# The first projection's matmuls as two row halves of the array, fifteen matmuls apart

## The chip, the cores and the metric

The kernel runs on one core of a Trainium2 chip. The metric is the time of one execution on the device in microseconds (us): the median of three runs of the kernel before is 665.21 us, the lowest 665.0 and the highest 665.22.

## What is computed

One decoder layer on 2048 tokens of width 1024 in float32: an RMS norm, one input projection to 2816 columns, two mixers side by side on its pieces (retention in chunks, and softmax attention in a window of 128 keys), a gate on each, an output projection, and the residual.

```python
h = rms_norm(x, norm_w)
proj = jnp.einsum('bsd,de->bse', h, w_in)
rq, rk, rv, rg, sq, sk, sv, sg = jnp.split(proj, offsets, axis=-1)
ro = group_norm(retention(rotary(rq), rotary(rk), rv)) * silu(rg)
so = sliding_window_attention(sq, sk, sv, q_norm_w, k_norm_w, sinks, rel_bias) * silu(sg)
x = x + jnp.einsum('bse,ed->bsd', concatenate([ro, so]), w_out)
```

The lines on the group norm and the concatenation stand here in short form.

## The kernel before

**Four large products.** The input projection is done in three pieces, of 2 x 512, 2 x 384 and 2 x 512 columns, and the output projection is a fourth of 2 x 512 columns. In the code they are the four calls of `products`, with the weights W2, W1, W3 and W4; "the first projection" is the call with W2 (lines 1585 to 1588). The 2048 tokens form eight pairs p of two chunks of 128 tokens. For each pair the product is a 2 x 2 by 2 x 2 block product (two token chunks and two halves of the contraction, times two halves of the contraction and two column halves), and it is made by Winograd's variant of Strassen's method, with seven block products m = 1 to 7 in the place of eight. So each call makes 7 x 8 = 56 block products.

**One block product.** A block product contracts over 512 rows in four steps k of 128, the height of the array. Each operand is split in two `fp32r` tiles, `hi` (the rounded value) and `lo` (the rest), and each step takes three matmuls: x hi by w hi, x hi by w lo, x lo by w hi (function `passes`). That makes 12 matmuls of 128 x 128 stationary values, 512 moving columns in the first projection, all into one PSUM bank, `acc`. ScalarE (ACT) makes `hi`, VectorE (DVE) makes `lo`. The results are combined by ACT and DVE out of PSUM: copied or added to sums in SBUF (`s`, `u`, `t`, `r`), lines 801 to 845. For m = 2 and m = 4 the matmuls go on in the bank in which m = 1 or m = 7 of the same pair lies.

**The order.** Class `Turns` lists the 56 block products of a call: the steps ((1, 2), (6), (5), (7, 4), (3)), within a step the pairs in groups of four (`FOURS`, the first projection), three (`THREES`, the output projection) or two (`TWOS`), within a group m by m. The place in the list is the block product's turn. Each operation is given to `Program.op` with what it reads and writes, its cost on the engine, and a due time in turns; `Program.emit` then takes operations one after another, for the engine that is free first, by due time and by free buffers, and writes each engine's queue in that order. `SHARE` says how many 512-wide tiles or PSUM banks each kind of buffer may hold at once: 11 for the split x (`x`), 19 for the split weights (`wh`), 5 banks for the first projection's `acc` (`first`). A buffer named `turn` is written by every block matmul, so that they stay in the list's order.

**The first eight turns.** Turns 0 to 3, (1, 0) to (1, 3), are written out with other tiles (`opening`), since they start while x is still being loaded; turns 4 to 7, (2, 0) to (2, 3), follow in the ordinary form. With 12 matmuls to a turn these are 96 matmuls. Turns 8 to 55 are 48 block products, 576 matmuls.

**What else TensorE does.** After the first projection, smaller matmuls stand between the block matmuls: transposes with `ident`, the attention logits (`m<-ks,qT`, tiles of 64 rows by 32 columns of the array), the attention values (`m<-pT,vn`, 32 by 64) and the retention steps (`m<-v,qk` and others, 64 by 64). These run in parts of the array, several at a time, and are in fp32: the profile shows each as two matmuls. None of them lies inside the first projection.

**GpSimd (POOL).** It makes only the factors of the attention's q and k norms, in two chains of sixteen small operations (`qk_norms`, lines 1310 to 1326), the first of which is due at turn 50.5.

Of the kernel before, what the change touches and what calls it, by code (L numbers as in the profile page):

```python
# [39 lines left out]
P = 128  # L40
NCH = S // P
NP = NCH // 2
HALF = P // 2
# [20 lines left out]
SHARE = {"x": 11, "raw": 92, "acc": 58, "wr": 28, "wh": 19, "att": 17, "ret": 35, "rin": 87, "gate": 25, "mix": 53, "norm": 14, "res": 7, "turned": 18, "vn": 3, "first": 5, "block": 3, "rest": 6}  # L64

AHEAD_OF = {"x": 5.0, "wh": 8.0}

# [17 lines left out]
OPENING = 4  # L85
SEM = 0.06
# [55 lines left out]
class Program:  # L142
# [5 lines left out]
    def op(self, cost, go, r=(), w=(), due=0.0, table=None, label="", also=(), many=0):  # L148


        o = Op()
        o.cost, o.go, o.due, o.after, o.set, o.label, o.many = cost, go, due + SHIFT.get(label, 0.0), [], table, label, many * MORE
        o.n, o.left, o.ready, o.end, o.seen, o.by = len(self.ops), 0, 0.0, 0.0, 0.0, None
        deps = set()
        for b in r:
            if b.writer is not None:
                deps.add(b.writer)
        for b in w:
            if b.writer is not None:
                deps.add(b.writer)  # L160
            deps.update(b.readers)
        for b in r:
            b.readers.append(o)
        for b in w:
            b.writer, b.readers = o, []
        o.bufs = list(dict.fromkeys((*r, *w, *also)))
        for b in o.bufs:
            b.left += 1
        o.new = [b for b in (*w, *also) if b.ap is None and b.tag]
        for d in deps:  # L170
            if d is not o:
                d.after.append(o)
                o.left += 1
        self.ops.append(o)
        return o
# [200 lines left out]

def f32r(n, count):
    t = count * (n / 2400 + 0.0135)
    return {"T": (t, t + 0.2, False)}


# [46 lines left out]
def layer(ctx, tc, xt, xfirst, xtok, nw, w_in, w_rn, qkw, sinks, biasg, rope, decays, dmask, gpow, w_out, out):  # L428
# [19 lines left out]
    op = prog.op  # L448
# [13 lines left out]
    def ps(share="rest", name="m"):  # L462
        return Buf("bank", None, F32, name, share)
# [51 lines left out]
    wr = fixed([P, 4], "wr")  # L515
# [237 lines left out]


    turn = Buf(name="turn", ap=())

    def products(B, W, n, base, seq, sink, plus=None, opening=None):


        s, u, t, bank = {}, {}, {}, {}  # L760

        def passes(m, acc, xh, xl, cols, k, d, goes_on, parts, which):


            wh, wl = W[m][k]

            def go(e):
                for i in which:
                    a, b = ((xh, wh), (xh, wl), (xl, wh))[i]
                    e.matmul(  # L770
                        acc()[:, :n], a()[:, cols], b()[:, :n], start=(not goes_on and k == i == 0),
                        stop=(k == 3 and i == 2), skip_group_check=goes_on,
                    )
# [3 lines left out]
            op(f32r(n, len(which)), go, reads, [acc, turn], d, label=f"product {m}", also=(xh, xl, wh, wl),  # L777
               many=2 * len(which))

        for m, p in seq.all:  # L780
            d = base + seq.at[m, p]
            goes_on = m in (2, 4)
            if plus and (m, p) == seq.all[-1]:
                last_product(B[m, p], W[m], d, t[p], p)
                break
            if not goes_on:
                bank[p] = ps("first" if opening else "block", "acc")
            acc = bank[p]
            if m > 1 or p >= OPENING or not opening:
                xh, xl = B[m, p]  # L790
                for k in range(4):
                    passes(m, acc, xh, xl, slice(k * P, (k + 1) * P), k, d, goes_on, (xh, xl), (0, 1, 2))
            elif p == OPENING - 1:
                for k, (xh, xl, parts) in enumerate(opening):

                    for which in ((0,), (1,), (2,)) if k < 3 else ((0, 1, 2),):
                        for q in range(OPENING):
                            due = (OPENING * k + q) / 4
                            passes(m, bank[q], xh, xl, slice(q * P, (q + 1) * P), k, due, False, parts[q // 2], which)

            def copy(dst, acc=acc, due=d - 3):
                op(
                    {"A": act(n)}, lambda e: e.activation(dst()[:, :n], acc()[:, :n], AF.Copy),
                    [acc], [dst], due, label="copy " + dst.name,
                )
                return dst

            def add(dst, a, acc=acc, due=d - 3):
                op(
                    {"V": dve(n)}, lambda e: e.tensor_tensor(dst()[:, :n], acc()[:, :n], a()[:, :n], ALU.add),  # L810
                    [acc, a], [dst], due, label="add " + dst.name,
                )
                return dst

            def more(dst, a, due):
                op(both(n), lambda e: e.tensor_tensor(dst(), dst(), a(), ALU.add), [dst, a], [dst], due, label="more")
                return dst

            if m == 1:
                if not opening or p >= OPENING:
                    s[p] = copy(kb("s", "acc"))
                elif p == OPENING - 1:
                    for q in range(OPENING):
                        s[q] = copy(kb("s", "acc"), bank[q], 2.6 + q)
            elif m == 2:
                r = plus(p, 0, 0, d) if plus else None
                sink(p, 0, 0, add(r, r) if plus else copy(kb("c", "acc")), d)
            elif m == 6:  # L830
                u[p] = add(s[p], s[p])
            elif m == 5:
                t[p] = add(kb("t", "acc"), u[p])
                if plus:
                    more(u[p], plus(p, 1, 0, d + 10), d + 10)
            elif m == 7:
                r = add(kb("r", "acc"), t[p])
                if plus:
                    r = more(plus(p, 1, 1, d), r, d + 1)
                    more(t[p], plus(p, 0, 1, base + seq.at[3, p] - 3), base + seq.at[3, p] - 3)  # L840
                sink(p, 1, 1, r, d)
            elif m == 4:
                sink(p, 1, 0, add(u[p], u[p]), d)
            else:
                sink(p, 0, 1, add(t[p], t[p]), d)

    def last_product(x, w, d, t, p):
# [717 lines left out]
    def go(e):  # L1565
        for _ in range(WARM):
            e.matmul(pw()[:, 0:256], zero.broadcast_to([P, P]), zero.broadcast_to([P, 256]), start=True, stop=True)
# [8 lines left out]
        label="no values",  # L1576
# [131 lines left out]
```

## Time and profile before

| | |
|---|---|
| median of three runs | 665.21 us (665.0 to 665.22) |
| span of the profiled execution | 663.5 us |
| TensorE (PE) busy | 658.8 us, 99% |
| its weight loads (PEld) | 562.3 us, 85% |
| VectorE (DVE) busy | 590.7 us, 89% |
| ScalarE (ACT) busy | 474.3 us, 71% |
| GpSimd (POOL) busy | 18.2 us, 3% |
| PE's granted clock, mean | 0.999 |

The profiled execution has a span of 663.5 us from its first to its last instruction; no total of its own is given for it, and the runs' median is 1.7 us above that span. PE is the matmul part of TensorE, PEld its weight loads, which overlap with matmuls. A row of the chain of waits gives start, length, what was done, and how many instructions; a row of the timeline the same with the engine first; a row of a table by window gives, for each engine, the busy time and in brackets the number of instructions that lie in it or touch it. Nearly every row names L424, the line of the helper through which each operation is issued, so groups are told apart by the tiles' names.

### The profile page before, as it was taken

Reading aid. Unit: us, or ns where it says so; the run is one execution under the profiler, and the core shown is the slowest. Engines: PE = TensorE matmul, PEld = TensorE weight load, DVE = VectorE, ACT = ScalarE, POOL = GpSimd, SP = SyncE. Lnnn points to the kernel's source line nnn. Section 1 sums busy time; section 2 is a strip of 40 time slices with the busy share of each in tenths; the row PEclk is TensorE's granted clock in tenths of the full one; section 3 lists DMA queues with packets and bytes.
Section 4 is the critical chain, followed back from the end, with each engine's and each line's share of the span. In section 5 each row is a group of like instructions: output and inputs, shape, how many; then the busy total and the mean of one; then the engine's idle time right before and its main releaser. Section 6 shows DMA issues by size and latency. Waiting matters only on the chain.

```text
span 663.5 us, 16277 instructions
## 1 busy us (share of the span) xinstructions
PE 658.8 (99%) x5952; PEld 562.3 (85%) x5952; DVE 590.7 (89%) x1369; ACT 474.3 (71%) x1154; POOL 18.2 (3%) x39
## 2 busy tenths in 40 slices
PE   9999999999999999999999999999999999999998
PEld 7888888889999999998878888877888888888887
DVE  6999977797799888899999999798999999998762
ACT  7665895567699676697999789899999863534200
POOL 0000000033300000000000000000000000000000
PEclk9999999999999999999999999999999999999999
DMA  9979997769949979999998999979977897146322
GB/s 319 385 234 314 317 324 252 241 211 332 220 156 284 276 230 310 286 295 313 296 214 255 256 263 259 244 211 258 299 238 218 226 198 215 45 162 212 137 95 96
DMA packets 152800, 160.86 MB, mean 242 GB/s; under 512 B 66704, under 2 KB 94224, under 8 KB 152720
## 3 DMA queue, kind: packets, MB, share of 16 engines
q1 hardware_dynamic: 152576, 159.81, 80.6%
q8 instruction: 47, 0.77, 0.5%
q14 instruction: 33, 0.27, 0.1%
q10 hardware_dynamic: 144, 0.00, 0.0%
HBM read 96.79 MB, written 49.09 MB: 220 GB/s over the span
## 4 chain that ended last, share of the span: by engine, by line
PE 99%; DMA 1%; ACT 0%; SPq 0%; DVE 0%; issue 0%
PE acc L424 88%; PE m L424 11%; DMA x<-in_xfirst 1%; ACT x L424 0%; SPq L424 0%; DVE t L424 0%
## 5 line engine op out<-in xcount | busy, mean ns | idle before, releaser
L424 PE MATMUL acc<-w,x 128*128 128x512 f32 (+1 forms) x2700 | 588.4, 377 | 0.9 <-ACT x L424 0.9
L424 PEld LDWEIGHTS acc<-w,x 128*128 128x128 f32 x2700 | 493.0, 188 | 84.4 <-issue 4.4
L424 DVE TENSOR_TENSOR x<-x 128x512 fp32r<-128x512 f32 (+2 forms) x220 | 143.6, 675 | 11.6 <-ACT x L424 10.5
L424 ACT ACTIVATE x<-x 128x512 fp32r<-128x512 f32 (+1 forms) x187 | 111.2, 620 | 21.3 <-DVE x L424 9.2
L424 ACT ACTIVATE lg<-lg,nm 128x160 f32<-128x160 f32 x128 | 53.1, 418 | 19.6 <-DVE nm L424 19.6
L424 DVE TENSOR_TENSOR w<-w 128x512 fp32r<-128x512 f32 (+3 forms) x96 | 61.1, 656 | 1.1 <-ACT w L424 1.1
L424 DVE SCALAR_TENSOR_TENSOR w<-w,nw_sb 128x512 fp32r<-128x512 f32 (+3 forms) x72 | 49.3, 702 | 0.9 <-ACT w L424 0.9
L424 DVE TENSOR_TENSOR s<-acc,s 128x512 f32<-128x512 f32 (+1 forms) x64 | 41.5, 649 | 8.3 <-PE acc L424 7.7
L424 ACT ACTIVATE w<-w 128x512 fp32r<-128x512 f32 (+1 forms) x72 | 41.3, 606 | 7.8 <-PE acc L424 5.1
L424 DVE CUSTOM_DVE_ANT_0 lg<-m,bias,nsnk 128x160 f32<-128x160 f32 x128 | 40.2, 379 | 2.3 <-PE m L424 2.2
L424 DVE TENSOR_TENSOR t<-acc,t 128x512 f32<-128x512 f32 (+2 forms) x33 | 21.0, 638 | 18.2 <-PE acc L424 18.0
L424 ACT ACTIVATE w<-w,nw_sb 128x512 fp32r<-128x512 f32 (+3 forms) x44 | 28.4, 691 | 3.3 <-DMA w<-in_w_in 2.3
L424 ACT ACTIVATE x<-go 128x512 fp32r<-128x512 f32 x27 | 16.8, 627 | 15.3 <-PE acc L424 7.5
L424 DVE TENSOR_TENSOR r<-acc,t 128x512 f32<-128x512 f32 (+1 forms) x32 | 20.8, 651 | 7.5 <-PE acc L424 7.2
L424 ACT ACTIVATE s<-acc 128x512 f32<-128x512 f32 (+1 forms) x32 | 18.3, 572 | 12.1 <-PE acc L424 11.5
L424 ACT ACTIVATE ro<-ro,nmu,rg 128x128 f32<-128x128 f32 x64 | 25.1, 481 | 2.1 <-DVE nmu L424 2.1
L424 DVE STREAM_TRANSPOSE pT<-lg 128x640 f32<-128x640 f32 x32 | 25.8, 825 | 0.9 <-ACT lg L424 0.9
L424 ACT ACTIVATION_READ_ACCUMULATOR lg<-lg,nm 128x1 f32 x128 | 24.3, 190 | 0.0
L424 DVE TENSOR_TENSOR t<-acc,s 128x512 f32<-128x512 f32 (+1 forms) x32 | 20.7, 645 | 3.8 <-PE acc L424 3.8
L424 ACT ACTIVATE xk<-xk 128x512 f32<-128x512 f32 x32 | 19.7, 620 | 4.3 <-DMA xk<-in_xtok 4.3
L424 ACT ACTIVATE qk<-qk,factors 128x64 f32<-128x64 f32 x64 | 16.9, 337 | 6.9 <-DVE qk L424 6.9
L424 ACT ACTIVATE ro<-m 64x256 f32<-64x256 f32 (+2 forms) x52 | 20.4, 392 | 0.6
(144 smaller groups left out, 590.6 us busy)
## 6 DMA issues: line engine op xcount, KB each, us to landing
x<-in_xt SPq DMA_DIRECT2D x80, 256.0 KB, 4.7
planes_dram<-apart SPq DMA_DIRECT2D x53, 256.0 KB, 3.6
x<-s_dram SPq DMA_DIRECT2D x46, 256.0 KB, 4.3
w<-in_w_in SPq DMA_DIRECT2D x40, 256.0 KB, 5.1
xk<-in_xtok SPq DMA_DIRECT2D x32, 256.0 KB, 4.9
res<-in_xtok SPq DMA_DIRECT2D x32, 256.0 KB, 3.5
s_dram<-x SPq DMA_DIRECT2D x23, 256.0 KB, 4.5
w<-in_w_out SPq DMA_DIRECT2D x20, 256.0 KB, 4.1
```

What stands on the lines that cost most here:

```text
L424: return lambda *a, **k: self.order.put(op(*a, **k))
```

## The change

In the first projection, from turn 8 to turn 55, each of the 576 block matmuls is issued as two matmuls, one on the upper 64 rows of the array (`rows` 1) and one on the lower 64 (`rows` 0), each over all 128 array columns and all 512 moving columns. A slot holds one upper matmul of the current block product and, fifteen matmuls behind it (`LAG`), one lower matmul of an earlier one. With 12 matmuls to a block product the lower half of a product starts three slots after its upper half has ended, so the two halves of a slot are always of different products and write to different banks. The upper half of a product clears the bank and the lower half adds to it. The first fifteen slots hold an upper half alone, and fifteen more slots at the end a lower half alone: 576 + 15 = 591 slots.

That the lower half of a product comes after its upper half is kept by a wait: a `nop` on GpSimd's queue (label `handed`) waits for the product's last upper matmul, and the first lower matmul waits for that `nop`. There are 48 of them.

Around it, the split weights get 20 tiles in the place of 19, and in the output projection's list the block product (3, 0) is moved ahead of (4, 6). Due times and costs being changed by this, `emit` puts some operations of later stages in other places as well. No operation is left out or added but the split matmuls and the `nop`s.

Three places in the queues, rows as the program has them (a name in brackets is the engine whose semaphore the instruction waits for; x9 stands for nine equal rows).

TensorE's queue at turn 8 of the first projection, before; `acc` is the bank, `w` and `x` the split operands:

```order
L424 MATMUL acc<-w,x 128x512 [waits Activation_49]
L424 MATMUL acc<-w,x 128x512
L424 MATMUL acc<-w,x 128x512 [waits DVE_49]
L424 MATMUL acc<-w,x 128x512 x9
L424 MATMUL acc<-w,x 128x512 [waits Activation_49]
```

The same place now:

```order
L436 MATMUL acc<-w,x 128x512 [waits Activation_49]
L436 MATMUL acc<-w,x 128x512
L436 MATMUL acc<-w,x 128x512 [waits DVE_49]
L436 MATMUL acc<-w,x 128x512 x9
L436 MATMUL acc<-w,x 128x512 [waits Activation_49]
L436 MATMUL acc<-w,x 128x512
L436 MATMUL acc<-w,x 128x512 [waits DVE_49]
L436 MATMUL acc<-w,x 128x512
L436 MATMUL acc<-w,x 128x512 [waits Pool_sequencer_49]
L436 MATMUL acc<-w,x 128x512 x16
L436 MATMUL acc<-w,x 128x512 [waits Activation_49]
L436 MATMUL acc<-w,x 128x512 x3
```

The first twelve are product 8's upper halves alone, then three upper halves of product 9; from there upper and lower halves alternate, and the first lower one has the new wait on GpSimd's sequencer. In all, 672 matmuls of 512 columns have become 1248 up to the first of 384 columns.

GpSimd's queue at the first chain of q and k norms (`hs` the sums of squares, `fac` the factors, `rqk0t` a scratch tile), before:

```order
L424 TENSOR_TENSOR hs_86<-hs_86,r_all 128x40 [waits DVE_49]
L424 TENSOR_SCALAR hs_86<-hs_86 128x40 [waits Pool_49]
L424 TENSOR_SCALAR fac_87<-hs_86 128x40 [waits Pool_49]
L424 TENSOR_TENSOR rqk0t<-fac_87 128x40 [waits Pool_49]
L424 TENSOR_TENSOR rqk0t<-rqk0t,hs_86 128x40 [waits Pool_49]
```

Now; a `nop` has no row of its own, its wait for PE stands with the next row:

```order
L436 TENSOR_TENSOR hs_86<-hs_86,r_all 128x40 [waits PE_49,DVE_49]
L436 TENSOR_SCALAR hs_86<-hs_86 128x40 [waits Pool_49]
L436 TENSOR_SCALAR fac_87<-hs_86 128x40 [waits Pool_49]
L436 TENSOR_TENSOR rqk0t<-fac_87 128x40 [waits PE_49,Pool_49]
L436 TENSOR_TENSOR rqk0t<-rqk0t,hs_86 128x40 [waits Pool_49]
L436 TENSOR_SCALAR rqk0t<-rqk0t 128x40 [waits Pool_49]
L436 TENSOR_TENSOR fac_87<-fac_87,rqk0t 128x40 [waits PE_49,Pool_49]
```

So 44 of the 48 `nop`s stand ahead of the chain's first operation and the last four inside the chain, three or four operations apart.

TensorE's queue in the output projection (`go` a gated result that is turned, `pT` and `vn` the attention weights and values), before:

```order
L424 MATMUL acc<-w,x 128x512 x42
L424 MATMUL m<-ident,go 128x128 x8
L424 MATMUL acc<-w,x 128x512 x9
L424 MATMUL m<-pT,vn 64x128 x32
L424 MATMUL m<-pT,vn 64x256 x8
L424 MATMUL m<-pT,vn 64x128 x32
L424 MATMUL acc<-w,x 128x512 x111
```

Now:

```order
L436 MATMUL acc<-w,x 128x512 x9
L436 MATMUL m<-pT,vn 64x128 x32
L436 MATMUL m<-pT,vn 64x256 x8
L436 MATMUL m<-pT,vn 64x128 x32
L436 MATMUL acc<-w,x 128x512 x63
L436 MATMUL m<-ident,go 128x128 x4
L436 MATMUL acc<-w,x 128x512 x492
```

The last attention values have moved from the start of this stage to 63 + 492 + 24 block matmuls ahead of the program's end (the last 24, of 384 and 128 columns, are unchanged).

The diff, cut to its core:

```diff
-SHARE = {"x": 11, ..., "wh": 19, ...}
+SHARE = {"x": 11, ..., "wh": 20, ...}
...
 class Turns:
-    def __init__(self, many):
+    def __init__(self, many, apart=False):
...
+        if apart:
+            self.all.remove((3, 0))
+            self.all.insert(self.all.index((4, groups[-1][0])), (3, 0))
...
-FOURS, THREES, TWOS = Turns(4), Turns(3), Turns(2)
+FOURS, THREES, TWOS = Turns(4), Turns(3, True), Turns(2)
...
+TILED = {0: (8, 56)}
+TILE_GAP = 0.0055
+LAG = 15
...
+        def piece(e, m, acc, x, cols, k, i, rows=None, goes_on=False, start=False, stop=False):
+
+            a, b = ((x[0], W[m][k][0]), (x[0], W[m][k][1]), (x[1], W[m][k][0]))[i]
+            r = slice(0, P) if rows is None else slice(rows * HALF, rows * HALF + HALF)
+            return e.matmul(acc()[:, :n], a()[r, cols], b()[r, :n], start=start, stop=stop, skip_group_check=goes_on or rows is not None)
...
+        def halves(slots, d):
...
+            for both_halves in slots:
+                for rows, j, q in both_halves:
+                    m, p = chain[j]
+                    x, w, (k, i) = B[m, p], W[m][q // 3], divmod(q, 3)
+                    made.append((j, q, (m, bank_of[j], x, slice(k * P, (k + 1) * P), k, i, rows, True,
+                                        rows == 1 and q == 0 and m not in (2, 4), rows == 0 and q == 11)))
...
+            def go(e):
+                for j, q, a in made:
+                    ins = piece(e, *a)
+                    if a[6] == 1 and q == 11:
+                        last[j] = ins
+                    elif a[6] == 0 and q == 0:
+                        behind(ins, last[j])
...
+        def handed(j, d):
+
+            def go(e):
+                ins = e.nop(nofuse=True)
+                behind(ins, last[j])
+                last[j] = ins
+
+            op({"G": (0.05, 0.2, False)}, go, [bank_of[j]], [relay], d, label="handed")
...
+            if first <= seq.at[m, p] < end:
+                j = seq.at[m, p] - first
+                bank_of.append(begin(m, p))
+                for q in (0, 3, 6, 9):
+                    of, k = range(q, q + 3), 12 * j + q - LAG
+                    halves([[(1, j, i)] + ([(0, *divmod(12 * j + i - LAG, 12))] if k >= 0 else []) for i in of], d)
+                    done(k + 2)
+                handed(j, d)
+                if j == len(chain) - 1:
+                    for k in range(12 * j + 12 - LAG, 12 * j + 12, 3):
+                        halves([[(0, *divmod(i, 12))] for i in range(k, k + 3)], d + 0.5)
+                        done(k + 2)
+                continue
```

`behind` adds a dependency with a semaphore between two instructions; `done` calls the code that empties a bank once its product's last lower matmul has been issued.

More of the change, by code (lines that the diff above doesn't have):

```diff
@@ L62 @@
 SMALL, COUNTS = 3, {"ms": 1, "rxt": 1, "rqk0t": 1, "rqk1t": 1, "state": 4, "sT": 2}
-SHARE = {"x": 11, "raw": 92, "acc": 58, "wr": 28, "wh": 19, "att": 17, "ret": 35, "rin": 87, "gate": 25, "mix": 53, "norm": 14, "res": 7, "turned": 18, "vn": 3, "first": 5, "block": 3, "rest": 6}
+SHARE = {"x": 11, "raw": 92, "acc": 58, "wr": 28, "wh": 20, "att": 17, "ret": 35, "rin": 87, "gate": 25, "mix": 53, "norm": 14, "res": 7, "turned": 18, "vn": 3, "first": 5, "block": 3, "rest": 6}
 AHEAD_OF = {"x": 5.0, "wh": 8.0}
@@ L378, in f32r, with tiled @@
     t = count * (n / 2400 + 0.0135)
+    return {"T": (t, t + 0.2, False)}
+def tiled(n, count):
+    t = count * (n / 2400 + TILE_GAP)
     return {"T": (t, t + 0.2, False)}
@@ L755, in layer, with behind, passes @@
     turn = Buf(name="turn", ap=())
+    relay = Buf(name="relay", ap=())
+    def behind(ins, other):
+        tc.add_manual_dep(
+            ins.ins, other.ins.name, mybir.DependencyInfo(mybir.DependencyClass.Sync, mybir.DependencyReason.DATA),
+            reason="one half of the rows after the other",
+        )
     def products(B, W, n, base, seq, sink, plus=None, opening=None):
         s, u, t, bank = {}, {}, {}, {}
-        def passes(m, acc, xh, xl, cols, k, d, goes_on, parts, which):
+        def piece(e, m, acc, x, cols, k, i, rows=None, goes_on=False, start=False, stop=False):
+            a, b = ((x[0], W[m][k][0]), (x[0], W[m][k][1]), (x[1], W[m][k][0]))[i]
+            r = slice(0, P) if rows is None else slice(rows * HALF, rows * HALF + HALF)
+            return e.matmul(acc()[:, :n], a()[r, cols], b()[r, :n], start=start, stop=stop, skip_group_check=goes_on or rows is not None)
+        def passes(m, acc, x, cols, k, d, goes_on, parts, which):
             wh, wl = W[m][k]
@@ L768, in go @@
                 for i in which:
[L769 to L773, printed above, removed]
+                    piece(e, m, acc, x, cols, k, i, None, goes_on, not goes_on and k == i == 0, k == 3 and i == 2)
             pairs = ((parts[0], wh), (parts[0], wl), (parts[1], wh))
@@ L776, in passes @@
             reads = list(dict.fromkeys(b for i in which for b in pairs[i]))
-            op(f32r(n, len(which)), go, reads, [acc, turn], d, label=f"product {m}", also=(xh, xl, wh, wl),
+            op(f32r(n, len(which)), go, reads, [acc, turn], d, label=f"product {m}", also=(*x, wh, wl),
                many=2 * len(which))
-        for m, p in seq.all:
-            d = base + seq.at[m, p]
[L782 to L799, printed above, removed]
@@ new lines, in halves @@
+        def halves(slots, d):
+            if not any(slots):
+                return
+            made, reads, writes = [], [], []
+            for both_halves in slots:
[4 more added lines that the diff above has]
+                                        rows == 1 and q == 0 and m not in (2, 4), rows == 0 and q == 11)))
+                    reads += (x[i == 2], w[i == 1])
+                    writes.append(bank_of[j])
+            def go(e):
[5 more added lines that the diff above has]
+                        behind(ins, last[j])
+            op(tiled(n, len(slots)), go, list(dict.fromkeys(reads)), [*dict.fromkeys(writes), turn], d,
+               label="product", many=2 * len(made))
@@ new lines, in handed, with done, begin @@
+        def handed(j, d):
[4 more added lines that the diff above has]
+            op({"G": (0.05, 0.2, False)}, go, [bank_of[j]], [relay], d, label="handed")
+        def done(k):
+            if k > 0 and k % 12 == 11:
+                finish(*chain[k // 12], bank_of[k // 12])
+        def begin(m, p):
+            if m not in (2, 4):
+                bank[p] = ps("first" if opening else "block", "acc")
+            return bank[p]
@@ L845, in products @@
                 sink(p, 0, 1, add(t[p], t[p]), d)
+        first, end = TILED.get(base // NP // 7, (len(seq.all), 0))
+        chain, bank_of, last = seq.all[first:end], [], {}
+        for m, p in seq.all:
+            d = base + seq.at[m, p]
+            if plus and (m, p) == seq.all[-1]:
+                last_product(B[m, p], W[m], d, t[p], p)
+                break
+            if first <= seq.at[m, p] < end:
[11 more added lines that the diff above has]
+                continue
+            acc, x, goes_on = begin(m, p), None, m in (2, 4)
+            if m > 1 or p >= OPENING or not opening:
+                x = B[m, p]
+                for k in range(4):
+                    passes(m, acc, x, slice(k * P, (k + 1) * P), k, d, goes_on, x, (0, 1, 2))
+            elif p == OPENING - 1:
+                for k, (xh, xl, parts) in enumerate(opening):
+                    for which in ((0,), (1,), (2,)) if k < 3 else ((0, 1, 2),):
+                        for q in range(OPENING):
+                            due = (OPENING * k + q) / 4
+                            passes(m, bank[q], (xh, xl), slice(q * P, (q + 1) * P), k, due, False, parts[q // 2], which)
+            finish(m, p, acc)
     def last_product(x, w, d, t, p):
```

1 line of the change is left out of this document (added).

## The prediction

> **What bounds the kernel now.** I read the page's busy shares first, then what TensorE waited for, then the chain of waits.
>
> ```profile
> PE 658.8 (99%) x5952; PEld 562.3 (85%) x5952; DVE 590.7 (89%) x1369; ACT 474.3 (71%) x1154; POOL 18.2 (3%) x39
> PE acc L424 <- ACT x L424: 0.9, 1, 0.9
> PE acc L424 88%; PE m L424 11%; DMA x<-in_xfirst 1%; ACT x L424 0%; SPq L424 0%; DVE t L424 0%
> ```
>
> TensorE is busy for 99% of the span, a block matmul waited once, for 0.9 us, and the chain that sets the end is TensorE's own work. So a microsecond taken from TensorE's stream comes off the time, unless something else is then late. What that stream costs is read from its uninterrupted stretches in the chain of waits (start, length, how many matmuls):
>
> ```profile
> 203.36 6.45 PE acc L424 x36
> 227.65 10.61 PE acc L424 x60
> 381.78 5.66 PE acc L424 x24
> 389.15 7.02 PE acc L424 x30
> ```
>
> The lower two are of 512 columns: six matmuls more take 1.36 us more, so one takes 226.7 ns, and 24 of them leave 5.66 - 5.44 = 0.22 us, which is what it costs to enter and leave work in parts of the array. The upper two are of 384 columns: 4.16 us for 24, 173.3 ns each. The difference, 53.4 ns for 128 columns, is 0.417 ns a column. So 512 columns stream for 213.4 ns, and each block matmul has **13.3 ns** on top, whatever its width. Only this part can shrink.
>
> The changed stretch is turns 8 to 55. Its end is found from the chain's first long piece, which holds the first projection and 24 matmuls of 384 columns, and ends at 161.95; less 24 x 0.173 and the 0.2 us of the change to the first transposition, that is 157.6 us, and 576 x 226.7 ns = 130.6 us earlier, 27.0, is the start. The windows:
>
> ```profile
> 5.19 156.76 PE acc L424 x696
> ...
> 27.04:80.00 52.96, 52.96 (x235) 43.89 (x234) 52.42 (x88) 34.79 (x76) 0.00 (x0) 1.00 0.88 294
> 80.00:157.60 77.60, 77.60 (x344) 64.28 (x343) 62.41 (x129) 52.27 (x129) 6.68 (x16) 1.00 0.81 274
> ```
>
> TensorE is busy in all of its 130.56 us, at full granted clock (1.00), and that is the 576 matmuls' own time: there is no wait in it.
>
> **The change, part by part.** *What goes:* 576 matmuls of 226.7 ns, 130.6 us.
>
> *What comes:* slots of two halves, if the halves run at the same time. Each half still streams 512 columns, so a slot is not under 213.4 ns. And the lag costs whole slots: fifteen with an upper half alone, fifteen with a lower half alone, so 576 + 15 = **591** slots. The fifteen extra ones cost 3.2 us by themselves. Since the halves stand in a part of the array, the stretch is entered and left once, another 0.22 us. The change gains only where the slot is under (130.6 - 0.2) / 591 = **220.6 ns**, that is, where the 13.3 ns shrink to under 7.2.
>
> No 64-row half over all columns in this number format is in the trace. The nearest rows are the retention steps: four tiles of 64 by 64 at a time, two row halves in different banks, a new weight load for each.
>
> ```profile
> 387.86 0.62 PE L424 MATMUL m<-v,qk 64*64 64x128 f32 x16
> 388.30 0.41 PE L424 MATMUL m<-qkT 64*64 64x64 f32 x16
> 388.53 0.62 PE L424 MATMUL m<-state,qkT 64*64 64x128 f32 x16
> ```
>
> From one row's start to the next, sixteen matmuls are four rounds of four: 0.44 / 4 = 110 ns for 128 columns, 0.23 / 4 = 57.5 ns for 64. The slope is 0.82 ns a column, about two column times of 0.417 for this format; that makes 106.8 and 53.4 ns of streaming, and 3 to 4 ns on top of a round. So row halves do run at the same time, and a round has little on top. It doesn't prove as much for the halves here, which stream twice as fast. I bound the slot from below by the 3 ns (216.4 ns) and from above by no shrinking at all (226.7). If what is on top goes with the rows of a tile, half of it is left, 6.6 ns. I take 4.9 ns, between 3 and 6.6, **218.3 ns**: 591 x 218.3 = 129.0, + 0.2 - 130.6 = **-1.4 us**. The ends: 591 x 216.4 + 0.2 - 130.6 = -2.5 us; 591 x 226.7 + 0.2 - 130.6 = +3.6 us.
>
> *The weight loads* double in number. What one costs alone shows at the end, where the stream is short:
>
> ```profile
> 659.18 1.28 PE L424 MATMUL acc<-w,x 128*128 128x128 f32 x10
> L424 PE MATMUL acc<-w,x 128*128 128x128 f32 x12 | 1.5, 271 | 0.0
> ```
>
> Ten matmuls from the first's start to the last's end, with a last one of 271 ns, leave (1.28 - 0.27) / 9 = 112 ns each, where 128 columns stream for 53: a load of 128 columns takes up to 112 ns of the array's time. Two in a row make 224 ns, over the stream. If the halves' loads can't overlap, the slot is 224 ns and the sum is 591 x 224 + 0.2 - 130.6 = +2.0 us. Against it: a round of the steps' 57.5 ns holds four loads of 64 columns. At half of 112 each these would take 224 ns one after another, so about four overlap, though over column halves too. The Trainium skill ("TensorE: Matmul & The Clock Gate", LDWEIGHTS) says that a load's time goes by columns and not by rows, 128 / 1.2 = 107 ns, so halving the rows shortens no load; that speaks against this change. By that figure two loads in a row are 213 ns, and the sum would stay at that of the stream. The trace agrees on the size, with its 112 ns.
>
> *The new wait.* The first lower half of each product waits for a `nop` on GpSimd, which waits for the product's last upper half. Behind it on TensorE stands everything. The rows that size it are a block matmul's mean time from start to end (392 ns), the last step of the chain, and GpSimd's first chain:
>
> ```profile
> L424 PE MATMUL acc<-w,x 128*128 128x512 f32 x2004 | 464.8, 392 | 0.9 <-ACT x L424 0.9
> 660.47 0.02 issue
> 660.50 0.29 DVE L424 TENSOR_TENSOR t<-acc,t 128x128 f32<-128x128 f32 x1 [0.73 <-PE acc L424]
> 143.06 0.55 POOL L424 TENSOR_TENSOR hs<-hs,r_all 128x40 f32<-128x40 f32 x1 [141.61 <-DVE hs L424]
> 143.70 0.54 POOL L424 TENSOR_SCALAR hs<-hs 128x40 f32<-128x40 f32 x1
> ...
> 150.47 0.50 POOL L424 TENSOR_TENSOR fac<-fac,rstd_all 128x40 f32<-128x40 f32 x1
> ```
>
> The last upper half starts in slot 11 and ends 0.39 us later; the lower one starts four slots after it, 0.87 us, and its weights should be loaded from one slot earlier, 0.65 us. That leaves 0.26 us for two hops. One hop is 0.03 us from TensorE to VectorE (660.47 to 660.50), and GpSimd takes 143.70 - 143.61 = 0.09 us to go on after its own result. Taking 0.03 + 0.09 + 0.03 = 0.15 us, it fits; I take nothing for it.
>
> *GpSimd's chain.* Four `nop`s stand between the operations of the first chain of norms, so TensorE waits if the chain is late, and the chain waits for TensorE. Three or four operations of some 0.46 us (sixteen from 143.06 to 150.47) are 1.9 us at most, and a turn of 12 slots is 2.6 us. The chain is faster than the turns, so TensorE doesn't wait. The chain itself now ends after the last turn, at the very end of the projection, not four us before. Its first reader on TensorE is a transposition 24 matmuls of 384 columns, 4.2 us, later; I take nothing.
>
> *Operands.* VectorE is busy 52.42 of 52.96 us between 27 and 80 us, and TensorE would ask for its work 3.8% faster. What covers this is its lead, seen at 65.12 us (27.04 + 14 turns of 2.72), where turn 22 begins:
>
> ```profile
> L424 DVE TENSOR_TENSOR x<-x x60: 415/679/693, 5.6 to 64.8; 128x512 f32<-128x512 f32 x30, 128x512 fp32r<-128x512 f32 x22, 128x256 fp32r<-128x256 f32 x8
> ```
>
> Of the split's second halves (fp32r), the eight small ones are turns 0 to 3 and the 22 large ones reach turn 25: over three turns, 8 us ahead. Twenty turns of 0.1 us and the 3.3 us for which tiles are now held longer don't use that up. If they did, the 240 slots before 80 us would gain nothing, 2.0 us less, and the sum would be +0.6.
>
> *Issue and SyncE's queue.* TensorE gets 1152 instructions more, a matmul and a load for each slot. The logits' stretch in the chain below holds 128 matmuls and their loads in 2.36 us, 18 ns a matmul; a slot of two needs 218 ns. In SyncE's queue the loads of the norm's tokens (`xk`) move behind some stores; before, the last is issued at 84.8 us, and the chain that needs their sums starts at 143.06. I take nothing for either.
>
> ```profile
> 201.00 2.36 PE m L424 x128
> L424 SPq DMA_DIRECT2D xk<-in_xtok x32: 327/382/1217, 48.3 to 84.8; - x32
> ```
>
> *The rest* is other places for the same work: the number of stretches in parts of the array is the same, so TensorE's own sum is too. The move of (3, 0) and of the last values can only add waits, and there were none.
>
> **The rivals.** *Nothing on top shrinks*: the 13.3 ns is the same at 512 and 384 columns, so it belongs to each matmul, and a half has it too. Then it is +3.6 us, 668.8. The tiled rounds speak against it. Chance 0.07.
>
> *The hop by GpSimd is late* (the other side): it decides from 0.26 us on, and each tenth beyond costs 48 x 0.1 = 4.8 us. At 0.1 us late it is -1.4 + 4.8 = +3.4, 668.6. For it: no row shows a TensorE wait on GpSimd. Against it: the hops above. Chance 0.07. Other new waits (operands, GpSimd's chain, the moved values): +0.6 to a few us, 0.07.
>
> *Loads in a row*, 224 ns: +2.0 us, 667.2, chance 0.05; partly overlapped, a slot of 219.5 to 222.8: within 0.2% of before, 0.10.
>
> *Halves in turn, not together*: twice 226.7 in 576 slots is 130 us more. Four tiles at once in a round of 110 ns speak clearly against it: 0.01.
>
> *The rounds' 3 ns hold here*: slots of 217.3 and less, -2.0 us and better, about 662.7 (the 3 ns end at -2.5). Chance 0.22.
>
> **How the numbers follow.** The forecast, slots of 217.3 to 219.5 ns and no new waits, has 0.41: -2.0 to -0.7 us, middle -1.4. The sum is against the profiled execution's span of 663.5 us, so 662.1; the runs' median lies 1.7 us above that span, and I add the change to it: 665.2 - 1.4 = **663.8 us**. A measurement of this kernel can tell about 0.2%, 1.3 us, from no change, so the forecast lies on that border, and half of it counts as faster. Faster: 0.21 + 0.22 = 0.43. Same: 0.20 + 0.10, and 0.04 of the other waits, 0.34. Slower: 0.07 + 0.07 + 0.05 + 0.01, and 0.03 of the other waits, 0.23. The range: below, -3.1 us, a slot of 215.4 (2 ns on top), 662.1; above, the loads in a row, 667.2. It leaves out the two rivals at +3.4 and +3.6, the halves in turn, and what lies beyond at either end, some 0.2 together.
>
> **What would show it.** The stretch from turn 8 should take some 129.2 us in place of 130.6, as 591 slots of about 218 ns: its first 384-column matmul at 156.3 us and not at 157.6. Fifteen matmuls at either end should stand alone at the same pace. TensorE's waits should show no GpSimd; GpSimd's first chain should end with the projection. Slots near 227 or 224, or a gap in each product's fourth slot, would make the prediction wrong.

## The result, and the profile after

The changed kernel takes **672.63 us** (median of four runs, 671.91 to 673.06), the kernel before beside it 665.22 us. The ratio is 1.0105, with a 95% interval of 1.0088 to 1.0122: 1% slower, where 663.8 us and a range up to 667.2 were forecast. The profiled execution took 672.75 us with a span of 671.0 us, 7.5 us more than before.

The busy shares and what TensorE waited for (us in total, times, longest), after:

```profile
PE 664.3 (99%) x6528; PEld 584.7 (87%) x6528; DVE 594.0 (89%) x1370; ACT 476.2 (71%) x1153; POOL 14.3 (2%) x39
```

```profile
PE m L436 <- DVE state L436: 1.1, 1, 1.1
PE m L436 <- issue: 0.8, 1, 0.8
...
PE acc L436 <- ACT x L436: 0.6, 2, 0.4
PE acc L436 <- DVE x L436: 0.3, 1, 0.3
```

TensorE is still busy for 99%, and its busy time has grown by 5.5 us (658.8 to 664.3). No row names GpSimd, but three kinds of wait are new: one for VectorE's `state`, one with no releaser ("issue"), and two for operands (of ACT's two, one stood at the start before).

**The changed stretch.** By windows, from the first half at 27.25 us to the first 384-column matmul at 161.17 us:

```profile
27.25:161.17 133.92, 133.92 (x1153) 130.39 (x1153) 116.90 (x216) 87.61 (x203) 4.67 (x16) 1.00 0.81 271
```

No wait, full clock, and 133.92 us for 591 slots: **226.6 ns a slot**, the old pace, not 218.3. The first 384-column matmul comes at 161.17 and not at 156.3; before, it came at 157.6. The timeline has the pace of halves in pairs (upper row of the fence) and of lower halves alone at the end:

```profile
39.85 110.49 PE L436 MATMUL acc<-w,x 64*128 64x512 f32 x972
157.89 3.35 PE L436 MATMUL acc<-w,x 64*128 64x512 f32 x14
```

972 halves are 486 pairs; less a matmul's own 0.39 us and the 0.17 us by which the second half of a pair follows the first, (110.49 - 0.39 - 0.17) / 485 = 226.7 ns a pair. Fourteen alone: (3.35 - 0.39) / 13 = 228 ns each. So two halves do run at the same time, as forecast, and one half alone takes as long as two, or as a whole matmul.

**GpSimd's chain**, three rows of it with the idle time ahead of them:

```profile
150.13 0.26 POOL L436 TENSOR_TENSOR rqk0t<-fac 128x40 f32<-128x40 f32 x1 [1.49 <-PE acc L436]
152.85 0.26 POOL L436 TENSOR_TENSOR rqk0t<-fac 128x40 f32<-128x40 f32 x1 [1.44 <-PE acc L436]
...
159.25 0.25 POOL L436 TENSOR_TENSOR fac<-fac,rstd_all 128x40 f32<-128x40 f32 x1
```

It waits for TensorE at the `nop`s and ends at 159.5 us, with the projection, as forecast; nobody waits for it.

**After the first projection** 671.0 - 161.17 = 509.8 us follow, where there were 663.5 - 157.6 = 505.9: 3.9 us more, for the same work. The timeline shows three places. The retention step at 431 us, after and then before:

```profile
431.18 0.67 PE L436 MATMUL m<-v,sT 64*64 64x128 f32 x16
431.67 0.62 PE L436 MATMUL m<-v,qk 64*64 64x128 f32 x16
432.11 0.41 PE L436 MATMUL m<-qkT 64*64 64x64 f32 x16
432.33 0.62 PE L436 MATMUL m<-state,qkT 64*64 64x128 f32 x16
434.06 0.63 PE L436 MATMUL m<-ident,ro 128*128 128x128 f32 x4 [1.10 <-DVE state L436]
```

```profile
433.22 0.62 PE L424 MATMUL m<-state,qkT 64*64 64x128 f32 x16
433.77 5.73 PE L424 MATMUL acc<-w,x 128*128 128x512 f32 x24
```

Before, block matmuls followed the step. Now transpositions do, in banks that VectorE still has to empty, and TensorE stands for 1.10 us. The chain of waits has what VectorE was at, and ACT's eleven operations on `ro` that it had waited for:

```profile
424.90 4.35 ACT ro L436 x11
...
431.98 1.20 DVE w L436 x2
433.18 0.40 DVE sT L436 x2
433.58 0.34 DVE state L436
433.92 0.14 issue
434.06 0.63 PE m L436 x4
```

Two splits of weights (`w`, 1.20 us) stand ahead of `sT` and `state` in VectorE's queue. That they are what makes the step late is read from this chain; no run moves them alone. The second place is the last attention values, 144 matmuls, after and then before:

```profile
533.02 2.22 PE L436 MATMUL m<-pT,vn 32*64 32x128 f32 x118
536.08 0.68 PE L436 MATMUL m<-pT,vn 32*64 32x128 f32 x26 [0.84 <-issue]
```

```profile
478.89 2.54 PE L424 MATMUL m<-pT,vn 32*64 32x128 f32 x144
```

3.74 us in the place of 2.54, with a stop of 0.84 us that nothing shown in the profile released. The third is the output projection, where two stops for operands of 0.38 and 0.27 us cost some 0.27 us more each: the overlap with the next matmul is lost (0.16 us: 0.39 less 0.23), and the first one after a stop takes 0.34 us to the next one's start (0.73 - 0.39 in the first row below), 0.11 longer than usual.

```profile
543.48 0.73 PE L436 MATMUL acc<-w,x 128*128 128x512 f32 x2 [0.38 <-ACT x L436]
544.49 1.88 PE L436 MATMUL acc<-w,x 128*128 128x512 f32 x7 [0.27 <-DVE x L436]
```

That is 1.2 for the values, 1.1 to 1.2 for the step and 1.2 for the operands, 3.5 to 3.6 of the 3.9 us.

### The profile page after: what moved, and what is told of

Its sections match the earlier page's. It is cut to its first block, busy times and chain, and to the rows that moved or that the text cites. A ratio compares the mean times of both kernels' runs of the same rounds, so it can differ in the third digit from the quotient of the medians.

```text
span 671.0 us, 17495 instructions
## 1 busy us (share of the span) xinstructions
PE 664.3 (99%) x6528; PEld 584.7 (87%) x6528; DVE 594.0 (89%) x1370; ACT 476.2 (71%) x1153; POOL 14.3 (2%) x39
## 4 chain that ended last, share of the span: by engine, by line
PE 92%; DVE 4%; ACT 2%; DMA 1%; issue 1%; SPq 0%; ACTq 0%
PE acc L436 83%; PE m L436 10%; ACT ro L436 1%; DVE x L436 1%; DVE w L436 1%; DVE st L436 0%; DMA w<-in_w_in 0%; DVE t L436 0%; DMA v<-aq_dram 0%; DVE go L436 0%; DVE state L436 0%; SPq L436 0%; ACT w L436 0%; DVE sT L436 0%; DVE tcos L436 0%
## 5 line engine op out<-in xcount | busy, mean ns | idle before, releaser
L436 PE MATMUL acc<-w,x 128*128 128x512 f32 (+2 forms) x3276 | 593.1, 378 | 0.9 <-ACT x L436 0.6
L436 PEld LDWEIGHTS acc<-w,x 128*128 128x128 f32 (+1 forms) x3276 | 515.4, 187 | 67.1 <-issue 4.7
L436 PE MATMUL m<-pT,vn 32*64 32x128 f32 (+1 forms) x1152 | 20.6, 285 | 0.8 <-issue 0.8
L436 PEld LDWEIGHTS m<-pT,vn 32*64 32x64 f32 x1152 | 18.4, 130 | 3.1 <-issue 1.8
```

The costliest lines, as they stand in the source:

```text
L436: return lambda *a, **k: self.order.put(op(*a, **k))
```

## Experiments

Two theories stand against each other for the stretch. **Per matmul:** what lies on top of the stream belongs to each matmul in a row of matmuls, whatever part of the array it uses, so halves can't shrink it. **Per phase or load:** it is made by loads or by the way in which the two halves follow each other, and could still be had. For the later 3.9 us: waits from the new order of the queues, against a consequence of the halves themselves.

### The halves put together again: a_full

All queues of ACT, VectorE, SyncE and GpSimd as in the changed kernel; TensorE issues whole matmuls in the place of the halves.

```diff
-                    ins = piece(e, *a)
-                    if a[6] == 1 and q == 11:
-                        last[j] = ins
-                    elif a[6] == 0 and q == 0:
-                        behind(ins, last[j])
+                    if a[6] == 1:
+                        ins = piece(e, *a[:6], None, True, a[8], q == 11)
+                        if q == 11:
+                            last[j] = ins
```

> The changed kernel's queues on VectorE, ScalarE, GpSimd and SyncE instruction by instruction, but TensorE's 576 block matmuls issued at full height (each where its upper half stood, the lower halves left out; the same result is computed). Main theory: each half keeps the 13.3 ns on top, so a slot is 226.7 ns and the halves cost 15 extra slots plus one entry, 3.6 us; so turns 8 to 55 go back to 130.6 us, and the time falls by at least 3.6 us, to 669.0 or less. What is left over 665.2 is the other order of the queues: 1.2 us of a retention step that waits for VectorE stays. The wait of 1.1 us inside the last attention values and the operand waits of 1.0 us after it stay if the order causes them (669.0), and go if they hang on where the reload of TensorE's instructions falls, since 1152 instructions less shift it by half a piece (about 666.5). Rival, the halves alone cost all of it: 665.2.

It took 668.33 us, 1.0044 of before (1.0028 to 1.0061): 4.3 us under the changed kernel, and 3.3 us above before. The window from the first changed matmul to the first of 384 columns:

```profile
27.55:158.11 130.56, 130.56 (x577) 108.15 (x576) 115.09 (x214) 87.85 (x202) 4.94 (x13) 1.00 0.83 278
```

```profile
PE m L436 <- DVE state L436: 1.1, 1, 1.1
PE m L436 <- issue: 0.9, 1, 0.9
...
PE acc L436 <- ACT x L436: 0.6, 2, 0.4
PE acc L436 <- DVE x L436: 0.3, 1, 0.3
```

The stretch is 130.56 us again, to the hundredth, and the later waits are still there, the one without a releaser in an earlier stretch of values (at 217.53 us and not at the last). The traced execution is the slowest of the four, 670.1 us. So the loss has two parts: the halves, 3.4 us in the stretch, and the order of the queues.

### 128 more instructions ahead: f_shift

```diff
-        for _ in range(WARM):
+        for _ in range(WARM - 2):
...
+        for _ in range(34):
+            e.matmul(pw()[0:32, 0:1], zero.broadcast_to([P, 32]), zero.broadcast_to([P, 1]), start=True, stop=True)
```

The extra matmuls stand ahead of everything and move the place of each later one in TensorE's instruction stream.

> The changed kernel with all queues as they are, but 128 TensorE instructions more ahead of the first block matmul (34 tiny warm-up matmuls in the place of two large ones), which moves every later reload of instructions by half a piece. Theory: the 1.1 us wait in the last attention values (named issue by the profile) is a reload that falls into them; it goes, and with it most of the 1.0 us for which two block matmuls wait for their operands just after: 670.3 or a little more if the start is later. Rival, the wait has to do with the values' own inputs: no change, 672.5.

It took 674.48 us (1.0142, 1.0127 to 1.0158). TensorE's waits, and the timeline's row for the last values:

```profile
PE m L436 <- DVE state L436: 1.1, 1, 1.1
...
PE acc L436 <- ACT x L436: 0.4, 1, 0.4
PE acc L436 <- DVE x L436: 0.3, 1, 0.3
```

```profile
535.55 2.56 PE L436 MATMUL m<-pT,vn 32*64 32x128 f32 x144
```

The stop without a releaser is gone and the values take 2.56 us. Some 2 us less were expected of the whole, and it takes 1.9 us more than the changed kernel: the longer warm-up puts the first changed matmul at 29.82 us in the place of 27.25, while what follows the projection falls from 509.8 to 508.5 us.

In the kernel with whole matmuls, which has 576 instruction pairs less, the stop stood in another stretch of the values (at 217.53 us, 0.94 us). What fits both is that TensorE ran out of instructions in a burst of short ones. The 16 KB packets of the instruction queue q8 become more with TensorE's instructions: 47 before, 51 in the changed kernel, 52 here. In the two bursts that stop, such a packet starts 0.65 and 0.11 us after the burst's start; in none of the other 94 bursts of values in the traces of this case does one start within the first microsecond. But the place in the instruction stream does not decide it alone: j_bf16 and j_cols64 below have the whole matmuls' queue on TensorE, and the same burst runs through in 2.53 and 2.54 us. So with one trace of each kernel it is not shown that the 128 instructions are what removed the stop. The waits for `state` and for the operands stayed, so the operand waits were no consequence of that stop.

### The true price in the plan: c_price

```diff
-TILE_GAP = 0.0055
+TILE_GAP = 0.0133
```

The plan reckons with 5.5 ns on top of each slot; here it reckons with 13.3. The instructions are the same, in the order that follows from the slower slots.

> The changed kernel planned with the measured price of a slot (13.3 ns on top in the place of 5.5), so that the order is made for the times that occur. Theory that the later waits come from an order made for a TensorE 4.7 us faster than it is: they go, and only the slots' 3.6 us are left, 668.8. Rival, any new order of this size brings waits of its own: anywhere from 668.8 to 673.

It took 668.83 us (1.0055, 1.004 to 1.007).

```profile
27.39:161.39 134.00, 134.00 (x1153) 131.53 (x1153) 117.65 (x218) 87.24 (x202) 5.63 (x16) 1.00 0.80 270
```

```profile
PE m L436 <- PEq L1774: 0.8, 1, 0.8
PE acc L436 <- ACT x L436: 0.3, 1, 0.3
```

The stretch is as long as in the changed kernel and all later waits are gone; what is left is of the start. Behind the projection 667.4 - 161.39 = 506.0 us follow, where there were 505.9 before. So the halves by themselves cost 3.8 us (3.4 in the stretch, and some tenths at the start, which differs from run to run: the first changed matmul stood between 26.6 and 27.7 us in runs with the same opening). That is the rival "nothing on top shrinks". The other 3.8 us, 672.63 - 668.83, came with the order that was planned at 5.5 ns. e_phase below, planned at 5.5 ns too, has waits of the same kinds (0.7 us for `state`, 5.5 us for operands, the start's 0.5 among them); the three d kernels, planned without halves, have none of the three. That the wrong price as such makes the waits, and not the chance of one order, rests on these six orders, and in e_phase the hop disturbs the plan as well.

### The other two edits alone: d_untiled, d_apart, d_wh20

```diff
-TILED = {0: (8, 56)}
+TILED = {}
```

That is the first; the second has 19 tiles for the split weights as well, the third leaves (3, 0) where it was.

> No block matmul is split; the change's two other edits stay (20 tiles for the split weights, the block product (3, 0) moved ahead in the output projection), and the order of the queues is planned for that. If these two edits cost nothing by themselves, and the waits seen after the change come from a plan that reckons with slots that are too fast, the time is that of the kernel before, 665.0 us, within 1 us. If one of the two edits makes waits (the operand waits stand in the output projection, where the second edit acts), it is 666 to 668, with a wait for operands at about 537 us.

> The kernel before with the block product (3, 0) of the output projection moved ahead, and nothing else. If this move makes the operand waits of the output projection, they show here and the time is 666 to 667 us; if not, it is 665.0 us.

> The kernel before with 20 tiles for the split weights in the place of 19, and nothing else. One tile more can only let splits start earlier: 665.0 us, or up to 1 us less if a split was late for it. If it moves operations in VectorE's queue ahead of what TensorE waits for, some tenths of a us more.

They took 665.23, 665.54 and 665.21 us, beside 665.4 for the kernel before: ratios of 0.9998 (0.9989 to 1.0007), 1.0003 (0.9994 to 1.0012) and 0.9995 (0.9986 to 1.0005). Neither of the two edits costs or gains anything that can be told. In the first one's trace:

```profile
PE acc L436 <- DVE r L436: 0.3, 1, 0.3
PE acc L436 <- ACT x L436: 0.2, 1, 0.2
```

A wait of 0.3 us, and none of the three places.

### The halves in step: e_phase

```diff
-LAG = 15
+LAG = 12
...
-                    halves([[(1, j, i)] + ([(0, *divmod(12 * j + i - LAG, 12))] if k >= 0 else []) for i in of], d)
+                    halves([([(0, *divmod(12 * j + i - LAG, 12))] if k >= 0 else []) + [(1, j, i)] for i in of], d)
```

The lower half of a product follows right behind its last upper half, so both halves of a slot wait for the hop by GpSimd and start together.

> The changed kernel with a lag of twelve and the lower half first in a slot, so that both halves of every product pair start together after a wait (in the changed kernel they run 57 and 170 ns apart). It costs a wait of some 0.4 us a product, so its time is about 20 us longer; what counts is the slot's length inside a product. Theory, the 13.3 ns belong to each matmul whatever runs beside it: 226.7 ns. Rival, they come from the two halves being out of step, and shrink when both start together: about 218 ns, as in the rounds of small tiles.

One run, 698.29 us. Four pairs inside a product, the weight loads after the hop, and what the loads waited for in all:

```profile
70.55 1.07 PE L436 MATMUL acc<-w,x 64*128 64x512 f32 x8
```

```profile
71.75 0.30 PEld L436 LDWEIGHTS acc<-w,x 64*128 64x128 f32 x4 [0.56 <-POOLq L436]
```

```profile
PEld acc L436 <- POOLq L436: 26.6, 48, 0.6
```

Inside a product a pair takes (1.07 - 0.39) / 3 = 227 ns, although both halves now start within 4 ns of each other. How the halves lie to each other is not the cause. The last halves end at 70.55 + 1.07 = 71.62 us and the next loads start at 71.75: **the hop takes 0.13 us**, where 0.15 was forecast. The loads stand idle for it 26.6 / 48 = 0.55 us a product. In the stretch, from 27.61 to 182.32 us, it costs less, since 588 slots of 226.7 ns are 133.3 us: (154.7 - 133.3) / 48 = 0.45 us a product. In the changed kernel it lies wholly in the three slots between.

### Four kinds of matmul: i_forms, j_bf16, j_cols64

All three ran once, with whole matmuls and the changed kernel's other queues; `piece` gets a kind, 0 to 3 for the four contraction steps of a product in the first, 1 throughout in the second, 2 for eleven of twelve in the third.

```diff
+            if kind == 0:
+                s, t = s.bitcast(F32), t.bitcast(F32)
+            elif kind == 1:
+                s, t = s.bitcast(BF16)[:, 1::2], t.bitcast(BF16)[:, 1::2]
+            elif kind == 2:
+                out, s = out[0:HALF], s[:, 0:HALF]
```

> The changed kernel's queues with the 576 matmuls unsplit, and in each block product of the changed stretch four kinds of three matmuls: the first three read their operands as plain fp32 (each then counts as two matmuls), the next three read the upper 16 bits of each value as bf16 (so part of each product is left out), the next three have 64 of the 128 stationary columns (half of that part is left out), the last three are as before. The start-to-start times inside each kind tell what the 13.3 ns on top of the stream belongs to. If it belongs to the number format of the split operands (fp32r): with 64 columns still 226.7 ns; plain fp32, whose transpositions of 128 columns have about 2 ns on top of 106.7, 427 + 2 = 429 ns for each of its two matmuls; bf16 213.4 ns with little on top, some 216 ns. If it belongs to a load of 128 stationary columns: 64 columns about 220 ns, plain fp32 427 + 13 = 440, bf16 226.7. If it belongs to every matmul of a stream: 226.7 with 64 columns, 440 and 226.7. The time of the whole, about 668 + 48 x 3 x (2 x 429 - 227) ns = 759 us, says nothing else.

It took 760.45 us, as such a mix should. Five of the plain fp32 matmuls in a row:

```profile
27.12 2.31 PE L437 MATMUL acc<-w,x 128*128 128x512 f32 x5
```

With a last one of 0.59 us, (2.31 - 0.59) / 4 = 430 ns; the records of the trace say 428.6. Two column times of 0.417 ns for 512 columns are 426.7, so plain fp32 has **2 ns on top over the whole array**. The bf16 ones were 225 to 228 ns apart, those with 64 columns 234; three in a row between other kinds are few, so both were run alone:

> The changed kernel's queues with the 576 matmuls unsplit, all on the upper 16 bits of each operand read as bf16 (what the low halves carry is partly left out). Three in a row between other kinds started 227.5 and 225 ns apart. If the 13.3 ns belong to the split format (fp32r) alone, 576 in a row go at about 216 ns each, the first of 384 columns is at about 151.5 us and the whole at about 662 us; if they belong to every matmul that streams a column in 0.417 ns, 226.7 ns each, the first of 384 columns at 157.6 us and the whole at the 668 us that these queues give with unsplit matmuls.

> The changed kernel's queues with the 576 matmuls unsplit, and all but the first of each block product's twelve with 64 of the 128 stationary columns: half of the product is left out. In a run of three between other kinds such matmuls started 230 to 234 ns apart; here eleven stand in a row. If what is on top of the stream goes with the load (64 columns loaded in half the time), the steady distance is about 220 ns; if it belongs to each matmul of this pace, 226.7 ns again, and what was above that between other kinds was the change of kind.

The windows over the 576 matmuls, bf16 and then 64 columns:

```profile
26.59:156.01 129.42, 129.42 (x577) 55.25 (x577) 114.77 (x214) 87.31 (x202) 4.94 (x13) 1.00 0.83 282
```

```profile
27.27:159.59 132.32, 132.32 (x577) 79.82 (x576) 115.30 (x214) 87.89 (x202) 4.94 (x13) 1.00 0.82 275
```

132.32 / 576 = **229.7 ns** with 64 columns, single steps between 223 and 237 (670.22 us as a whole). With bf16 129.42 / 576 = 224.7 ns; the last of these steps, to a matmul in another format, is recorded with 0.03 us only, and without it a step is (129.42 - 0.03) / 575 = **225.0 ns** (667.05 us as a whole). So what is on top doesn't shrink with the columns loaded, and of 13.3 ns 11.6 stay without the split number format: of two statements in my expectations, "the format" fell to bf16, and "the load" fell to the 64 columns and to the halves, which have two loads in a slot and the same pace. Only matmuls that stream at half the pace, plain fp32, have little on top. The Trainium skill ("TensorE: Matmul & The Clock Gate", "Wait — 56ns, not 53.3ns?") gives 215.7 ns for warm matmuls of 512 columns back to back, 2.5 ns on top. Measured here in bf16, with a weight load for each matmul and every second 16-bit value read, are 225.0 ns; the measurement decides.

## Why the prediction was wrong, point by point

**The step that failed** is the slot: "I take 4.9 ns, between 3 and 6.6, 218.3 ns", with its ends of 216.4 and 226.7. It measured 226.6, the upper end. The nearest rows were the retention steps, whose rounds have 3 to 4 ns on top, and I read this as a property of tiles. Those rows are fp32. The trace of before held the control that I didn't look for, plain fp32 over the whole array, four transpositions of 128 columns:

```profile
524.91 0.60 PE L424 MATMUL m<-ident,go 128*128 128x128 f32 x4
```

With a last one of 0.27 us, (0.60 - 0.27) / 3 = 110 ns each, 3 ns above 106.7: a whole tile has as little on top as a round of four. So the rounds said nothing about parts of the array; they differ from the block matmuls in the pace at which they stream. The 512 columns of i_forms show the same with a longer stream (2 ns). "If what is on top goes with the rows of a tile, half of it is left" was refuted by the first fifteen halves alone. The rival "nothing on top shrinks", with its argument that 13.3 ns were the same at 512 and 384 columns, was right to 0.2 us (+3.6 forecast, +3.8 by c_price, of which some tenths are the start's) and had a chance of 0.07; the rows that spoke against it should have been worth much less.

**The second term, sized at nothing:** "The move of (3, 0) and of the last values can only add waits, and there were none." 3.9 us of waits came. A stop inside a burst of values (1.2 us; the line on issue took nothing, from a burst that ran through), the order in VectorE's queue at one retention step (1.1 to 1.2) and two operand waits (1.2) were not looked at, although each operation's place behind the changed stretch had been planned anew. The two edits themselves are harmless (the d runs); the order planned at the forecast's price for a slot has these waits, and planned at the measured price it has none (c_price). The rival "other new waits" had up to a few us and a chance of 0.07, and the forecast had no case with both losses together, which is what happened.

**What held:** the two halves run at the same time; 591 slots; the loads are hidden, 130.39 us of them beside 133.92 us of matmuls, so "loads in a row" at 224 ns is not what is seen (a lone half with one load takes 227 as well); the hop of 0.15 us measured 0.13 and delayed nobody; GpSimd's chain ended with the projection (its operations come 0.49 us apart before, (150.47 - 143.06) / 15, and not 0.46, which changes nothing); VectorE's lead in the first projection was enough (no wait in the stretch). The fifteen slots at either end cost 15 x 226.7 = 3.4 us, and that is all that the halves did to the stretch.

**What stays open:** why a matmul at this pace has 12 to 16 ns on top and one at half the pace 2. Also open is what starts a stop inside a burst. Rows, columns, number format, phase and width were tried; a row of matmuls that share one weight load was not. No version here beats the kernel before: the best three, with whole matmuls, can't be told from it.

## What to carry to other kernels

Before a cost is ascribed to tiling, look for the same operation untiled and in the same number format: one such row in the trace of before would have shown that fp32 alone made the rounds cheap. Splitting a matmul that already fills the array gains only if the cost on top shrinks with the part, and a lag between the parts costs whole slots whatever happens. And where a planner sets the order, a wrong price for one stage can be paid in the later ones: give it the measured one and plan again before judging the change.

## What the runs showed of the hardware that I had not expected

- A matmul of 512 columns at a column per 0.417 ns comes every 226.7 ns with 128 rows, with 64, with two times 64 at once in either phase; 229.7 ns with 64 stationary columns; 225.0 ns in bf16. In plain fp32 it comes every 428.6 ns, 2 ns above its stream.
- A burst of 288 short instructions (144 matmuls and their loads in 2.5 us) stood still for 0.84 and 0.94 us in two of the 96 such bursts in these traces, the two in whose first microsecond a 16 KB packet of the instruction queue starts.
- After a stop, the first matmul takes some 0.1 us longer to the next (0.34 us in the place of 0.23 after the wait for an operand at 543 us, 0.33 after the hop in e_phase).
